# Block 1's attention maps in pairs of half-row matmuls, masks on VectorE, heads one chunk apart

## The chip, the core and the metric

The kernel runs on one core of a Trainium2 chip. The metric is the device time of one execution in microseconds. TensorE (PE, with its weight loads shown apart as PEld), VectorE (DVE), ScalarE (ACT), GpSimd (POOL) and the DMA queue of SyncE (SP) run side by side, each in its own order, and wait for each other on semaphores.

## The reference

Two transformer blocks follow each other on 256 tokens of 1024 features, all in fp32. Block 1 has two attention branches. The first is a differential attention with 4 heads: each head has two causal softmax maps over keys of 64 features, and the second is subtracted from the first, times a scalar. The second has 8 heads of 64 features; with 256 tokens in one block of 256 it is plain causal attention. Block 2 (two layers) has a retention branch with 4 heads and a stick-breaking branch with 8 heads of 128 features, and a feed-forward part.

```python
# Block 1, branch 0, for each of 4 heads and two maps m of 64 features
s = einsum('bqhmd,bkhmd->bhmqk', q, k) * scale ; s = where(key <= query, s, -inf)
a = softmax(s) ; w = a[:, :, 0] - lam * a[:, :, 1] ; o = w @ v
# Block 1, branch 1, for each of 8 heads of 64 features
s = einsum('bhqd,bhkd->bhqk', q, k) * scale ; s = where(key <= query, s, -inf) ; o = softmax(s) @ v
# Block 2, stick-breaking, for each of 8 heads and 2 layers
z = q @ k.T * scale ; causal = key < query ; lb = log_sigmoid(z) ; l1 = where(causal, lb - z, 0)
w = where(causal, exp(lb + reversed_cumsum(l1) - l1), 0) ; o = w @ v
```

## The kernel before, in words

All weights stream from HBM in 189 chunks of 128 x 2048 numbers (1 MB). fp32 numbers are split into a high and a low fp32r part (`split` for the weights: the high part on ACT, L286, the low part on DVE, L287; `hilo` for activations, L127 and L128), and a product is made of three matmuls, high by high, high by low and low by high (`mm3`, L131 to L133). A chunk of the main stream is 16 matmuls with 512 moving columns (L295) and 16 with 256 (L297), which fill one PSUM bank for each half of the chunk. The banks of the main stream are a ring of five (`acc`), those of everything else a ring of three (`aux`).

The main loop (L1007 to L1020) goes over the chunks. For chunk i it writes down the split of chunk i+2, the load of chunk i+5, then the matmuls and evacuations of chunk i, and after these one step (`next`) of every thread that was alive before chunk i. A thread is a Python generator; each `yield` puts what follows it one chunk later. This is a program order, not the order of execution: a planner with its own cost model takes, for each engine, from what is ready, and may move instructions of a later chunk ahead of those that wait. Only ScalarE's table functions (exp, sigmoid, ln) and its table loads keep the program's order among themselves, through the token in `act` (L107 to L115): when a function of the other table set comes next in program order, a table load stands before it.

`block1_branch(br)` (L546) makes q (2 chunks), k (2 chunks) and v (2 chunks) of one branch, and starts four `soft_head` threads (L462) when k is done. Each thread has two maps: in branch 0 the two maps of one head, in branch 1 two heads. The 64 features of map 0 lie on partitions 0 to 63, those of map 1 on 64 to 127. The steps of a thread:

- scores: for map 0 and then for map 1, six matmuls over 64 rows (three with 128 columns for the first 128 queries, three with 256 for the second) into a bank of `aux`, and a seventh matmul, `mask` (L458), that adds the causal mask to the two diagonal blocks by multiplying an identity with a table of 0 and -1e30. Then, for each map and each half of the queries, the maximum on DVE (L479), read from PSUM, and the exponential on ACT (L480, recorded as L114), read from PSUM. DVE makes the reciprocals and scales the result (L486, L487 in branch 0, L491 in branch 1).
- one chunk later, the turn: transposes on PE (L497) and `hilo` into the rings `ph` and `pl`.
- one chunk later, the product with v: in branch 0 nine matmuls with 128 columns (L509), then a norm of the head's output, and one chunk later a last transpose; in branch 1 six matmuls with 256 columns and six with 128 (L528, L529). The result goes to tile `A` (a1), multiplied with the gate tile `G` (g1).

Threads j = 0 and 1 take their scores two chunks behind the end of k, threads 2 and 3 three chunks behind. The program order of Block 1 is: branch 0 (chunks 0 to 5), the four gate chunks of both branches (6 to 9, `gate1`, whose sigmoids stand at chunks 7, 8 and 9), branch 1 (10 to 15), four more gate chunks (16 to 19), and at chunk 20 the first of the chunks that merge the branches (`branch1`, L611): its first half reads heads 0 to 3 of `A`, its second half heads 4 to 7. The gates wait for it in a ring of four buffers (`sig`).

In Block 2, `sb_head` (L746) uses the same `mask` helper with another table: six matmuls over 128 rows, then the mask matmul, then ACT's |z| from PSUM (L755).

Of the kernel before, what the change touches and what calls it, by code (L numbers as in the profile page):

```python
# [17 lines left out]
P = 128  # L18
# [3 lines left out]
S = 256  # L22
# [11 lines left out]
C_MQ = 704  # L34
C_MS = 832
C_TRI = 960
C_DEC = 1088
# [39 lines left out]
def tile_blocks(ctx: ExitStack, tc: tile.TileContext, a: dict, out: bass.AP):  # L77
# [66 lines left out]
    msk = tl([384], "sig", bufs=4)  # L144
# [8 lines left out]
    idr = tl([P], "idr", F32R)  # L153
    mqr = tl([P], "mqr", F32R)
    msr = tl([P], "msr", F32R)
# [7 lines left out]
    def late_consts():  # L163
        load(cst, a["tables"][:, 0:C_SB])
        load(msk, a["tables"][:, C_SB:C_DEC])
        load(lamv, a["lambdas"].rearrange("(o i e) -> o i e", o=1, e=64).to_broadcast([P, 4, 64]))

    def use_consts():
        V.tensor_mul(gfm, g_fin, g_mix[0])
        V.tensor_scalar_mul(subg, subg, 1.0 - LAM_INIT)  # L170
        V.tensor_copy(idr, ident)
        V.tensor_copy(mqr, msk[:, 0:128])
        V.tensor_copy(msr, msk[:, 128:256])
        V.tensor_copy(tri, msk[:, 256:384])
# [40 lines left out]
    def sums(sq, cols=True):  # L215
        h, l = tl([S], "ph", F32R, 4), tl([S], "pl", F32R, 4)
# [199 lines left out]
    e_slot = [scr[:, i * 768:(i + 1) * 768].rearrange("p (m q) -> p m q", m=2) for i in range(2)]  # L416
    o_slot = [scr[:, 1536 + i * 256:1536 + (i + 1) * 256].rearrange("p (h e) -> p h e", h=2) for i in range(2)]
# [37 lines left out]
    def mask(ps, m):  # L455

        o = ps.rearrange("p (b s) -> p b s", b=2)[:, :, 0:P]
        T.matmul(o, lhsT=idr, rhs=m[:, None, :].to_broadcast([P, 2, P]), start=False, stop=True, skip_group_check=True)  # L458

    BLK = ((0, 0, 0), (128, 1, 0), (256, 1, 1))  # L460

    def soft_head(idx, j, v, diff, wait):  # L462
# [3 lines left out]
        ps = [aux(), aux()]  # L466
        for m in range(2):
            r = slice(m * 64, m * 64 + 64)
            for o, q0, kn in ((0, 0, 128), (128, 128, 256)):
                q, k = slice(q0, q0 + 128), slice(0, kn)  # L470
                mm3(ps[m][:, o:o + kn], qh[r, q], ql[r, q], kh[r, k], kl[r, k], o == 0, False)
            mask(ps[m], mqr)
        e = e_slot[idx % 2]
        mx, sm = tl([4], "mx", bufs=4), tl([4], "sm", bufs=4)
        segs = ((0, 0, 128), (1, 128, 384))
        for m in range(2):
            for h, lo, hi in segs:
                i = 2 * m + h
                V.tensor_reduce(mx[:, i:i + 1], ps[m][:, lo:hi], AX.X, ALU.max, negate=True)  # L479
                act(e[:, m, lo:hi], ps[m][:, lo:hi], AF.Exp, bias=mx[:, i:i + 1], accum_out=sm[:, i:i + 1])  # L480
        rs = tl([4], "rs", bufs=4)
        V.reciprocal(rs, sm)
        if diff:
            V.tensor_scalar_mul(rs[:, 2:4], rs[:, 2:4], lam[:, 2:3])
            for h, lo, hi in segs:
                V.tensor_scalar_mul(e[:, 1, lo:hi], e[:, 1, lo:hi], rs[:, 2 + h:3 + h])  # L486
                V.scalar_tensor_tensor(e[:, 0, lo:hi], e[:, 0, lo:hi], rs[:, h:h + 1], e[:, 1, lo:hi], ALU.mult, ALU.add)  # L487
        else:
            for m in range(2):
                for h, lo, hi in segs:  # L490
                    V.tensor_scalar_mul(e[:, m, lo:hi], e[:, m, lo:hi], rs[:, 2 * m + h:2 * m + h + 1])  # L491
        yield
        wt = []
        for m in range(1 if diff else 2):
# [3 lines left out]
            h, l = tl([384], "ph", F32R, 4), tl([384], "pl", F32R, 4)  # L498
            hilo(h, l, pt[:, 0:384])
            wt.append((h, l))  # L500
# [3 lines left out]
        if diff:  # L504
            po = aux()[:, 0:S].rearrange("p (h e) -> p h e", h=2)
            h, l = wt[0]
# [16 lines left out]
        else:  # L523
            po = aux().rearrange("p (m q) -> p m q", m=2)
            for m in range(2):
                h, l = wt[m]
                vc = slice(j * P, (j + 1) * P)
                mm3(po[:, m], vh[:, 0, vc], vl[:, 0, vc], h[:, 0:256], l[:, 0:256], m == 0, False)  # L528
                mm3(po[:, m, 128:256], vh[:, 1, vc], vl[:, 1, vc], h[:, 256:384], l[:, 256:384], False, True)  # L529
# [16 lines left out]
    def block1_branch(br):  # L546
        v = Norm()
        for w_ in range(2):
            qn = []

            def qk_evac(ps, h, w_=w_, qn=qn):
# [8 lines left out]
                if w_:  # L560
                    for j in range(4):
                        threads.append(soft_head(4 * br + j, j, v, br == 0, 1 + j // 2))
# [16 lines left out]
    block1_branch(0)  # L579
    for c, b in enumerate((6, 7, 14, 15)):  # L580
        gate1(c, b)
    block1_branch(1)
# [128 lines left out]
    def ret_head(h, j, qk, v, L):  # L711
# [7 lines left out]
        dh, dl = tl([384], "ph", F32R, 4), tl([384], "pl", F32R, 4)  # L719
# [26 lines left out]
    def sb_head(h, j, qk, v, L):  # L746
# [4 lines left out]
        mm3(z[:, 256:384], kh[:, j, 128:256], kl[:, j, 128:256], qh[:, j, 128:256], ql[:, j, 128:256], False, False)  # L751
        mask(z, msr)
# [6 lines left out]
        h_, l_ = tl([384], "ph", F32R, 4), tl([384], "pl", F32R, 4)  # L759
# [7 lines left out]
        h_, l_ = tl([384], "ph", F32R, 4), tl([384], "pl", F32R, 4)  # L767
# [316 lines left out]
```

## Time and profile before

| | |
|---|---|
| time, median of 3 runs | 1178.29 us (1177.98 to 1181.79) |
| the profiled execution's own time | 1178.23 us |
| span of its trace | 1176.4 us |
| PE busy | 1161.2 us, 99% |
| DVE busy | 886.9 us, 75% |
| ACT busy | 706.7 us, 60% |
| granted TensorE clock | 0.996 of full speed |

The span reaches from the first to the last instruction of the program; 1.8 us of the profiled execution lie around it. A matmul's end in the trace is modelled and matmuls overlap, so what a matmul costs is read from the start of one to the start of the next, not from its duration.

### The profile page before, as it was taken

The numbers are of one execution on the slowest core, as the hardware profiler recorded it, in microseconds if no ns is written. First come the engines' busy times: TensorE is split into PE (matmuls) and PEld (weight loads), VectorE is DVE, ScalarE is ACT, GpSimd is POOL, SyncE is SP. The second block draws the span as 40 slices with busy tenths as digits, with TensorE's granted clock in tenths as the row PEclk, the third lists the DMA queues.
The fourth block names the chain that finished last, engine by engine and source line by source line (L and its number), as shares of the span: only waits on it lengthen the run. The fifth ranks groups of instructions, "written<-read, shape, count | busy, mean of one in ns | idle before, by whom it ended". The sixth has DMA issues, their size and how long they took to land.

```text
span 1176.4 us, 17442 instructions
## 1 busy us (share of the span) xinstructions
PE 1161.2 (99%) x6642; PEld 1011.3 (86%) x6642; DVE 886.9 (75%) x1449; ACT 706.7 (60%) x1275; POOL 230.4 (20%) x242
## 2 busy tenths in 40 slices
PE   8999999999999999999999999999999999999997
PEld 6888889997888888888888888888888888888887
DVE  6776768878989676568977777997776667867664
ACT  6657556566457776546745546556867565856452
POOL 1023104124462122202000002653112222000001
PEclk9999999999999999999999999999999999999999
DMA  8443434545335444545555555445444555555540
GB/s 309 180 143 144 146 114 160 202 180 203 144 143 179 148 163 155 190 169 185 209 191 203 180 185 217 162 161 182 159 145 157 190 191 192 184 182 199 192 179 36
DMA packets 29603, 204.47 MB, mean 174 GB/s; under 512 B 3408, under 2 KB 3664, under 8 KB 5584
## 3 DMA queue, kind: packets, MB, share of 16 engines
q1 hardware_dynamic: 29376, 203.34, 48.0%
q8 instruction: 52, 0.85, 0.3%
q14 instruction: 31, 0.25, 0.1%
q10 hardware_dynamic: 144, 0.03, 0.0%
HBM read 202.31 MB, written 1.05 MB: 173 GB/s over the span
## 4 chain that ended last, share of the span: by engine, by line
PE 93%; DVE 5%; issue 1%; ACT 0%; DMA 0%; POOL 0%; POOLq 0%; DVEq 0%; ACTq 0%
PE acc L295 41%; PE acc L297 21%; PE acc L336 19%; PE aux L131 2%; PE aux L133 2%; PE aux L132 1%; PE acc L131 1%; PE acc L132 1%; PE acc L133 1%; DVE wl L287 1%; DVE sig L801 1%; PE aux L458 1%; PE aux L764 1%; PE acc L324 1%; DMA X<-in_xt_dram 0%
## 5 line engine op out<-in xcount | busy, mean ns | idle before, releaser
L287 DVE TENSOR_TENSOR wl<-raw,wh 128x1024 fp32r<-128x1024 f32 (+1 forms) x380 | 463.2, 1253 | 154.4 <-ACT wh L286 152.2
L295 PE MATMUL acc<-X,wh 128*128 128x512 f32 x1472 | 524.7, 398 | 2.5 <-DVE vl L387 1.8
L286 ACT ACTIVATE wh<-raw 128x1024 fp32r<-128x1024 f32 (+1 forms) x380 | 380.7, 1047 | 200.2 <-PE acc L295 131.8
L297 PE MATMUL acc<-X,wl 128*128 128x256 f32 x1472 | 412.6, 281 | 0.0
L295 PEld LDWEIGHTS acc<-X,wh 128*128 128x128 f32 x1472 | 276.6, 188 | 64.5 <-DVE vl L387 2.1
L297 PEld LDWEIGHTS acc<-X,wl 128*128 128x128 f32 x1472 | 278.5, 189 | 2.3
L336 PE MATMUL acc<-wh,X 128*128 128x512 f32 x432 | 112.2, 392 | 0.0
L313 ACT ACTIVATE f<-acc 128x256 f32<-128x256 f32 x216 | 78.7, 372 | 42.2 <-PE acc L297 42.0
L314 DVE TENSOR_TENSOR f<-f,acc 128x256 f32<-128x256 f32 x216 | 86.4, 413 | 22.1 <-ACT f L313 21.3
L336 PEld LDWEIGHTS acc<-wh,X 128*128 128x128 f32 x432 | 79.7, 188 | 15.9
L295 PE MATMUL acc<-A,wh 128*128 128x512 f32 x256 | 90.2, 396 | 0.0
L295 PE MATMUL acc<-B,wh 128*128 128x512 f32 x256 | 90.1, 396 | 0.0
L207 POOL TENSOR_TENSOR sq<-sq,f 128x256 f32<-128x256 f32 x30 | 31.5, 1050 | 268.2 <-ACT f L205 267.6
L589 POOL TENSOR_TENSOR sig<-f,nr 128x256 f32<-128x256 f32 x48 | 42.5, 893 | 148.5 <-DVE f L314 148.4
L297 PE MATMUL acc<-B,wl 128*128 128x256 f32 x256 | 71.4, 279 | 0.0
L297 PE MATMUL acc<-A,wl 128*128 128x256 f32 x256 | 71.3, 279 | 0.0
L295 PE MATMUL acc<-M,wh 128*128 128x512 f32 x192 | 67.1, 397 | 0.0
L658 DVE TENSOR_TENSOR X<-X,acc 128x256 f32<-128x256 f32 x112 | 45.3, 416 | 24.8 <-PE acc L297 23.7
L336 PE MATMUL acc<-wl,X 128*128 128x512 f32 x216 | 59.5, 393 | 0.0
L295 PEld LDWEIGHTS acc<-B,wh 128*128 128x128 f32 x256 | 48.1, 188 | 11.6
L295 PEld LDWEIGHTS acc<-A,wh 128*128 128x128 f32 x256 | 48.1, 188 | 11.3
L297 PE MATMUL acc<-M,wl 128*128 128x256 f32 x192 | 52.7, 280 | 0.0
(224 smaller groups left out, 1744.6 us busy)
## 6 DMA issues: line engine op xcount, KB each, us to landing
raw<-in_wstream_dram SPq DMA_DIRECT2D x187, 1024.0 KB, 4.8
raw<-in_wstream_dram SPq DMA_DIRECT2D x4, 512.0 KB, 7.7
B<-in_tables_dram SPq DMA_DIRECT2D x2, 768.0 KB, 6.8
X<-in_xt_dram SPq DMA_DIRECT2D x2, 512.0 KB, 6.3
out_dram<-M SPq DMA_DIRECT2D x4, 256.0 KB, 2.2
M<-in_g_final_dram SPq DMA_DIRECT2D x1, 512.0 KB, 3.7
cst<-in_tables_dram SPq DMA_DIRECT2D x1, 352.0 KB, 10.0
B<-in_pt_dram SPq DMA_DIRECT2D x1, 256.0 KB, 2.7
```

What stands on the lines that cost most here:

```text
L131: T.matmul(o, lhsT=lh, rhs=rh, start=start, stop=False, skip_group_check=True)
L133: T.matmul(o, lhsT=ll, rhs=rh, start=False, stop=stop, skip_group_check=True)
L207: (V if k == KT - 1 else G).tensor_add(sq, sq, t)
L286: A.activation(ch.wh[:, k], ch.raw[:, k], AF.Copy)
L287: V.tensor_sub(ch.wl[:, k], ch.raw[:, k], f32(ch.wh[:, k]))
L295: T.matmul(ps, lhsT=ch.wh[:, k, w], rhs=x.rearrange("p c t -> p (c t)"), start=i == 0, stop=last, skip_group_check=True)
L297: T.matmul(ps[:, 0:S], lhsT=ch.wl[:, k, w], rhs=x[:, 0], start=False, stop=last, skip_group_check=True)
L313: A.activation(t, ps[:, S:2 * S], AF.Copy)
L314: V.tensor_add(t, t, ps[:, 0:S])
L336: T.matmul(p[:, 0:w], lhsT=xs[:, k, t], rhs=ws[:, i, o], start=n == 0 and k == 0, stop=n == 2 and k == KT - 1, skip_group_check=True)
L589: G.tensor_mul(store[(c, i)][0][:, k % 2], fold(ps), st.n.rb)
L658: V.tensor_add(X[:, k], X[:, k], ps[:, o:o + S])
```

## The change

- Scores: the masks' matmuls go. The twelve half-row matmuls of a thread are written as six pairs, map 0 and map 1 in turn, with the same columns, and a token keeps them in this order among themselves. Map 0 goes into an `aux` bank, map 1 into an `acc` bank.
- DVE's maximum becomes one instruction that reads the scores from PSUM and the mask from SBUF, adds them, changes the sign, writes the result to SBUF and gives the minimum of it. The exponential reads that result in SBUF, in place.
- The scaling of the exponentials goes from DVE to ACT (24 instructions; the four threads' `scalar_tensor_tensor` of branch 0 stay).
- Thread j waits 1 + j chunks, not 1 + j // 2, and there is a second `yield` between scores and turn. Four slots for the exponentials instead of two.
- Branch 1's product with v: both maps in one matmul, three with 512 and three with 256 columns.
- The rings `ph` and `pl` have two buffers of 768 instead of four of 384.
- Program order of Block 1: branch 0, two gate chunks (6, 7), branch 1 (8 to 13), two gate chunks (14, 15), and on as before.
- Block 2's stick-breaking: the mask matmul becomes an addition in PSUM on DVE; `h2`, `l2` hold both of a head's splits.

```diff
     def late_consts():
         load(cst, a["tables"][:, 0:C_SB])
-        load(msk, a["tables"][:, C_SB:C_DEC])
+        load(msk, a["tables"][:, C_SB:C_TRI])
+        load(tri_f, a["tables"][:, C_TRI:C_DEC])
...
-    def mask(ps, m):
-
-        o = ps.rearrange("p (b s) -> p b s", b=2)[:, :, 0:P]
-        T.matmul(o, lhsT=idr, rhs=m[:, None, :].to_broadcast([P, 2, P]), start=False, stop=True, skip_group_check=True)
...
         qh, ql, kh, kl = m1.h[:, j], m1.l[:, j], m1.h[:, 4 + j], m1.l[:, 4 + j]
-        ps = [aux(), aux()]
-        for m in range(2):
-            r = slice(m * 64, m * 64 + 64)
-            for o, q0, kn in ((0, 0, 128), (128, 128, 256)):
-                q, k = slice(q0, q0 + 128), slice(0, kn)
-                mm3(ps[m][:, o:o + kn], qh[r, q], ql[r, q], kh[r, k], kl[r, k], o == 0, False)
-            mask(ps[m], mqr)
-        e = e_slot[idx % 2]
+        ps = [aux(), acc()]
+        for o, q0, kn in ((0, 0, 128), (128, 128, 256)):
+            for n, (q_, k_) in enumerate(((qh, kh), (qh, kl), (ql, kh))):
+                for m in range(2):
+                    r = slice(m * 64, m * 64 + 64)
+                    mm = T.matmul(ps[m][:, o:o + kn], lhsT=q_[r, q0:q0 + 128], rhs=k_[r, 0:kn],
+                                  start=o == 0 and n == 0, stop=n == 2, skip_group_check=True)
+                    tc.stamp_issue_order_token(mm.ins, "maps")
+        e = e_slot[idx % 4]
...
-                V.tensor_reduce(mx[:, i:i + 1], ps[m][:, lo:hi], AX.X, ALU.max, negate=True)
-                act(e[:, m, lo:hi], ps[m][:, lo:hi], AF.Exp, bias=mx[:, i:i + 1], accum_out=sm[:, i:i + 1])
+                em = e[:, m, lo:hi]
+                V.tensor_tensor_reduce(em, ps[m][:, lo:hi], m_seg[h], -1.0, 3e38, ALU.add, ALU.min, mx[:, i:i + 1])
+                act(em, em, AF.Exp, scale=-1.0, bias=mx[:, i:i + 1], accum_out=sm[:, i:i + 1])
...
-                V.tensor_scalar_mul(e[:, 1, lo:hi], e[:, 1, lo:hi], rs[:, 2 + h:3 + h])
+                A.activation(e[:, 1, lo:hi], e[:, 1, lo:hi], AF.Copy, scale=rs[:, 2 + h:3 + h])
...
-                    V.tensor_scalar_mul(e[:, m, lo:hi], e[:, m, lo:hi], rs[:, 2 * m + h:2 * m + h + 1])
-        yield
-        wt = []
+                    A.activation(e[:, m, lo:hi], e[:, m, lo:hi], AF.Copy, scale=rs[:, 2 * m + h:2 * m + h + 1])
+        yield
+        yield
+        wh, wl = tl([2, 384], "ph", F32R, 2), tl([2, 384], "pl", F32R, 2)
...
-            for m in range(2):
-                h, l = wt[m]
-                vc = slice(j * P, (j + 1) * P)
-                mm3(po[:, m], vh[:, 0, vc], vl[:, 0, vc], h[:, 0:256], l[:, 0:256], m == 0, False)
-                mm3(po[:, m, 128:256], vh[:, 1, vc], vl[:, 1, vc], h[:, 256:384], l[:, 256:384], False, True)
+            vc = slice(j * P, (j + 1) * P)
+            mm3(po, vh[:, 0, vc], vl[:, 0, vc], wh[:, :, 0:256], wl[:, :, 0:256], True, False)
+            mm3(po[:, :, 128:256], vh[:, 1, vc], vl[:, 1, vc], wh[:, :, 256:384], wl[:, :, 256:384], False, True)
...
-                        threads.append(soft_head(4 * br + j, j, v, br == 0, 1 + j // 2))
+                        threads.append(soft_head(4 * br + j, j, v, br == 0, 1 + j))
...
-    block1_branch(0)
-    for c, b in enumerate((6, 7, 14, 15)):
-        gate1(c, b)
-    block1_branch(1)
+    for br, gates in ((0, (6, 7)), (1, (14, 15))):
+        block1_branch(br)
+        for c, b in enumerate(gates):
+            gate1(2 * br + c, b)
...
-        mask(z, msr)
+        zd = z.rearrange("p (b s) -> p b s", b=2)[:, :, 0:P]
+        V.tensor_add(zd, zd, m_sb)
```

## Rows read from the trace of the kernel before

**Rows 1.** The page: busy time, share of the span and instructions of each engine.

```profile
PE 1161.2 (99%) x6642; PEld 1011.3 (86%) x6642; DVE 886.9 (75%) x1449; ACT 706.7 (60%) x1275; POOL 230.4 (20%) x242
```

**Rows 2.** The page: the chain that ended last, by engine.

```profile
PE 93%; DVE 5%; issue 1%; ACT 0%; DMA 0%; POOL 0%; POOLq 0%; DVEq 0%; ACTq 0%
```

**Rows 3.** Busy time by stretch: stretch, length, PE, PEld, DVE, ACT, POOL, clock, DMA, GB/s.

```profile
44.00:125.00 81.00, 81.00 (x443) 67.72 (x443) 59.35 (x115) 53.67 (x124) 16.87 (x21) 1.00 0.42 148
125.00:180.00 55.00, 54.15 (x352) 47.38 (x351) 35.67 (x80) 30.96 (x73) 5.19 (x8) 1.00 0.32 114
260.00:360.00 100.00, 95.84 (x527) 82.21 (x525) 91.87 (x148) 58.85 (x103) 51.50 (x49) 0.98 0.43 159
360.00:440.00 80.00, 80.00 (x474) 70.74 (x472) 60.12 (x93) 59.10 (x111) 13.17 (x18) 1.00 0.45 160
```

**Rows 4.** PE in order of time, one map: start, duration, line, operation, tiles, rows*columns.

```profile
58.02 0.39 PE L295 MATMUL acc<-X,wh 128*128 128x512 f32 x1
58.34 0.32 PE L131 MATMUL aux<-M 64*128 64x128 f32 x1
58.50 0.27 PE L132 MATMUL aux<-M 64*128 64x128 f32 x1
...
59.02 0.28 PE L133 MATMUL aux<-M 64*128 64x256 f32 x1
59.22 0.38 PE L458 MATMUL aux<-mqr,idr 128*128 128x256 f32 x1
59.45 0.28 PE L297 MATMUL acc<-X,wl 128*128 128x256 f32 x1
59.56 0.40 PE L295 MATMUL acc<-X,wh 128*128 128x512 f32 x1
59.80 0.28 PE L297 MATMUL acc<-X,wl 128*128 128x256 f32 x1
```

**Rows 5.** PE in order of time where a map is broken up by the main stream.

```profile
50.54 0.32 PE L131 MATMUL aux<-M 64*128 64x128 f32 x1
50.79 0.38 PE L297 MATMUL acc<-X,wl 128*128 128x256 f32 x1
...
51.34 0.32 PE L132 MATMUL aux<-M 64*128 64x128 f32 x1
```

**Rows 6.** Block 1's mask line: count, shortest, median and longest ns, first and last start.

```profile
L458 PE MATMUL aux<-mqr,idr x16: 382/384/387, 52.1 to 156.7; 128*128 128x256 f32 x16
```

**Rows 7.** PE in order of time around a mask of Block 2.

```profile
371.28 0.27 PE L133 MATMUL aux<-M 128*128 128x128 f32 x1
371.39 0.33 PE L458 MATMUL aux<-msr,idr 128*128 128x256 f32 x1
371.56 0.28 PE L131 MATMUL aux<-M 128*128 128x256 f32 x1
```

**Rows 8.** PE in order of time, branch 1's product with v, idle time and releaser in brackets.

```profile
158.49 0.28 PE L133 MATMUL aux<-ph,vl 128*128 128x128 f32 x1
159.49 0.39 PE L131 MATMUL aux<-ph,vh 128*128 128x256 f32 x1 [0.73 <-ACT B L114]
...
160.93 0.30 PE L497 MATMUL aux<-cst,B 128*128 128x128 f32 x1
```

**Rows 9.** ACT and DVE by line and shape, 44 to 180 us: count, busy us, mean ns.

```profile
L479 DVE TENSOR_REDUCE mx<-aux 128x1 f32<-128x256 f32 x16 | 6.7, 417 | 3.5 <-ACT B L114 3.5
L112 ACT ACT_TABLE_LOAD x3 | 3.8, 1283 | 0.1
L517 ACT ACTIVATE B<-aux,ss 128x128 f32<-128x128 f32 x8 | 2.4, 387 | 1.3 <-POOL ss L515 1.3
L555 ACT ACTIVATE sig<-acc,nr 128x256 f32<-128x256 f32 x4 | 1.7, 474 | 1.3 <-PE acc L336 1.3
```

**Rows 10.** ACT in order of time around a table load.

```profile
82.63 1.28 ACT L112 ACT_TABLE_LOAD   x1
83.93 1.34 ACT L114 ACTIVATE f<-G 128x256 f32<-128x256 f32 x4
```

More of the change, by code (lines that the diff above doesn't have):

```diff
@@ L33 @@
 C_SB = 704
[L34 to L37, printed above, removed]
+C_Z = 704
+C_MQ = 832
+C_MS = 960
+C_TRI = 1088
+C_DEC = 1216
 C_ALL = C_DEC + 4 * 384
@@ L143, in tile_blocks @@
     cst = tl([C_SB], "cst")
-    msk = tl([384], "sig", bufs=4)
+    msk = tl([384], "msk")
+    tri_f = tl([P], "sig", bufs=4)
     ident = cst[:, C_ID:C_ID + P]
@@ L152, in tile_blocks @@
     V.tensor_copy(one_r, ones)
-    idr = tl([P], "idr", F32R)
-    mqr = tl([P], "mqr", F32R)
-    msr = tl([P], "msr", F32R)
+    m_seg = msk[:, P:2 * P], msk[:, 0:2 * P]
+    m_sb = msk[:, None, 2 * P:3 * P].to_broadcast([P, 2, P])
     tri = tl([P], "tri", F32R)
@@ L170, in use_consts @@
         V.tensor_scalar_mul(subg, subg, 1.0 - LAM_INIT)
[L171 to L174, printed above, removed]
+        V.tensor_copy(tri, tri_f)
         V.tensor_scalar_mul(neg1, ones, -1.0)
@@ L215, in sums @@
     def sums(sq, cols=True):
-        h, l = tl([S], "ph", F32R, 4), tl([S], "pl", F32R, 4)
+        h, l = tl([S], "ph", F32R, 2), tl([S], "pl", F32R, 2)
         hilo(h, l, sq)
@@ L415, in tile_blocks @@
     pw = scr[:, 2048:].rearrange("p (k t) -> p k t", k=KT)
-    e_slot = [scr[:, i * 768:(i + 1) * 768].rearrange("p (m q) -> p m q", m=2) for i in range(2)]
-    o_slot = [scr[:, 1536 + i * 256:1536 + (i + 1) * 256].rearrange("p (h e) -> p h e", h=2) for i in range(2)]
+    e_slot = [scr[:, i * 768:(i + 1) * 768].rearrange("p (m q) -> p m q", m=2) for i in range(4)]
+    o_slot = [scr[:, 3072 + i * 256:3072 + (i + 1) * 256].rearrange("p (h e) -> p h e", h=2) for i in range(2)]
     def start1():
@@ L497, in soft_head @@
                 T.transpose(pt[:, o:o + P], e[:, m, o:o + P], ident)
-            h, l = tl([384], "ph", F32R, 4), tl([384], "pl", F32R, 4)
-            hilo(h, l, pt[:, 0:384])
-            wt.append((h, l))
+            hilo(wh[:, m], wl[:, m], pt[:, 0:384])
         yield
@@ L505, in soft_head @@
             po = aux()[:, 0:S].rearrange("p (h e) -> p h e", h=2)
-            h, l = wt[0]
+            h, l = wh[:, 0], wl[:, 0]
             vc = slice(j * P, (j + 1) * P)
@@ L718, in ret_head @@
         V.tensor_mul(t, ps[:, 0:384], L.dec[:, 384 * h:384 * (h + 1)])
-        dh, dl = tl([384], "ph", F32R, 4), tl([384], "pl", F32R, 4)
+        dh, dl = tl([384], "ph", F32R, 2), tl([384], "pl", F32R, 2)
         hilo(dh, dl, t)
@@ L750, in sb_head @@
         mm3(z[:, 0:256], kh[:, j, 0:128], kl[:, j, 0:128], qh[:, j], ql[:, j], True, False)
-        mm3(z[:, 256:384], kh[:, j, 128:256], kl[:, j, 128:256], qh[:, j, 128:256], ql[:, j, 128:256], False, False)
-        mask(z, msr)
+        mm3(z[:, 256:384], kh[:, j, 128:256], kl[:, j, 128:256], qh[:, j, 128:256], ql[:, j, 128:256], False, True)
+        zd = z.rearrange("p (b s) -> p b s", b=2)[:, :, 0:P]
+        V.tensor_add(zd, zd, m_sb)
         zz = z[:, 0:384]
@@ L758, in sb_head @@
         V.scalar_tensor_tensor(t, zz, 0.0, t, ALU.max, ALU.add)
-        h_, l_ = tl([384], "ph", F32R, 4), tl([384], "pl", F32R, 4)
+        h2, l2 = tl([2, 384], "ph", F32R, 2), tl([2, 384], "pl", F32R, 2)
+        h_, l_ = h2[:, 0], l2[:, 0]
         hilo(h_, l_, t)
@@ L766, in sb_head @@
         act(t, zz, AF.Exp)
-        h_, l_ = tl([384], "ph", F32R, 4), tl([384], "pl", F32R, 4)
+        h_, l_ = h2[:, 1], l2[:, 1]
         hilo(h_, l_, t)
```

## The prediction

> **What bounds the kernel now.** I read the page first: PE is busy 99% of the span, DVE 75%, ACT 60% [rows 1]. Then the chain that ended last: 93% of it is PE [rows 2]. So the span is PE's work plus its few gaps, and a change is worth what it takes from PE's row of starts. Then busy time by stretch [rows 3]. Block 1's attention lies between 44 and 180 us; there PE has no idle time up to 125 us and 0.85 us of 55 after it, at full clock, while DVE is busy 95.0 of the 136 us (59.35 + 35.67) and ACT 84.6 (53.67 + 30.96). From 260 to 360 us, which the change hardly touches, DVE is busy 92 of 100 us and PE waits 4 us; from 360 to 440 us, where stick-breaking runs, PE has no idle time and DVE is busy 75%. Last I read PE in order of time, start to start, because the ends are modelled.
>
> **Maps, before.** One map's six matmuls and its mask take from 58.34 to 59.45, 1.11 us, and the way in costs 0.08 more: 58.02 to 58.34 is 0.32, while a 512-column matmul of the stream takes 0.24 (59.56 to 59.80) [rows 4]. That is 1.19 us. Block 1 has 16 such maps [rows 6]: 19.0 us. In three of them (starts near 50.5, 67.9 and 127.6) the planner put other matmuls inside; in the first, 0.80 us go from 50.54 to 51.34 [rows 5] for two stream matmuls (0.24 + 0.12) and a step of 0.16, so a break costs 0.28; three are 0.8. Sum 19.8 us.
>
> **Maps, after.** The mask, its way in (59.02 to 59.22, 0.20 for a matmul that else takes 0.12) and the second entry of each thread go. What is left are six pairs, one entry (0.08) and one exit (0.08). No pair of matmuls on different halves of the rows stands in this trace. Bounds: if the second of a pair costs nothing, a pair takes one step of 0.12 [rows 4], a thread 6 x 0.12 + 0.16 + 0.1 for the first start = 1.0 us, eight threads 8 us: 11.8 saved. If the two go one after the other at the 0.12 that half-row matmuls show, it is 12 x 0.12 + 0.16 = 1.6, eight 12.8: 7.0 saved. If each still pays what the first step shows (0.16 [rows 4]), 2.1, eight 16.6: 3.2 saved. I take the first end, 11.8: a stream matmul with 256 columns also takes 0.12 on all 128 rows (59.45 to 59.56 is 0.11), so the step is set by something other than the 128 columns of a small map, and the two halves share neither rows nor bank. It is a choice, so the second end is a rival.
>
> The Trainium skill (TensorEngine Tiling (Array Packing), Tiling Modes, Key Properties) says that tiles on different rows load weights and multiply in parallel; no run here shows it yet, and by it the saving is 11.8 us. The same section says that a change of tiling mode drains the engine; the 0.20 on the way from a map to its mask against 0.12 agrees [rows 4].
>
> **The other PE work.** Block 2's mask costs 0.17 us (371.39 to 371.56 [rows 7]); 8 heads in 2 layers make 16: 2.7 us. Branch 1's product with v takes 1.44 us in a thread (159.49 to 160.93 [rows 8]); after, three matmuls of 0.24 and three of 0.12 make 1.08: 0.36 by 4 threads, 1.4 us. PE's wait before it (158.49 to 159.49, less a matmul's 0.11 [rows 8]) ends on an exponential that still held an `aux` bank; the new maximum frees the bank on DVE, with one `aux` bank to a thread: 0.9 us goes, and nothing else is late there, as the main stream has two more chunks between k and the merge.
>
> **What is added.** All of it lies beside PE. DVE: the new maximum reads a mask too; lower bound the old 0.42 us, upper bound two passes, 0.83 [rows 9], I take 0.5; the 24 scalings that leave DVE outweigh it. Sixteen additions in PSUM of 128 x 256 at about 0.42 [rows 9] are 6.7 us over two stick-breaking stretches, in front of |z| on ACT; behind each addition stand splits and folds on DVE, and PE waits for the head only a chunk later. Cover: DVE's 25% idle [rows 3]; without it 3.3 us in each layer. ACT: 24 scalings, 12 of 0.39 and 12 of at most 0.47 [rows 9], 10.3 us. ACT's order also changes: exponentials of threads 2 and 3 of branch 0 now follow the sigmoids of chunk 7, and those of branch 1's threads 1 and 2 fall behind the sigmoids of chunks 14 and 15. Going through the program order I count seven table loads where there are three [rows 9]; four more at 1.28 are 5.1 us. ACT then has 84.6 + 10.3 + 5.1 = 100 us in a stretch of some 122: 82%. Cover is that threads turn two chunks behind their scores; the price without it is rival 3. The exponentials read SBUF instead of PSUM; I take no difference (between -0.1 and +0.1 us each, 3 us of ACT either way).
>
> The Trainium skill (ScalarE: Activation LUTs, What ACT_TABLE_LOAD costs) speaks against this order: it puts a switch at about 2.66 us with its drain. Here the load takes 1.28 and the next activation starts 0.02 us after its end [rows 10], so the row decides; by the page ACT would have 5.5 us more, and the sum would not move while the cover holds.
>
> **Nothing, with what hides it.** One load of constants more on SP's queue ahead of chunk 4's: 64 KB, at 148 GB/s [rows 3] 0.4 us, for a chunk that PE needs four chunks later. An `acc` bank goes to a map for the time to its last maximum, so the stream has four for some 3 us; the stream evacuates one bank while it fills the next. The rings `ph` and `pl` of two hold one thread in its turn and one at its product; in Block 2 a pair of heads fills both, and the next pair comes chunks later: at most one product of wait (1.4) in a few places.
>
> **The sum.** 11.8 + 2.7 + 1.4 + 0.9 = 16.8, less 0.8 for as many new breaks in maps as before: 16 us. The profiled execution took 1178.23 us, 1.8 around its span of 1176.4, and stands 0.06 from the median of 1178.29. Forecast **1162 us**, 1.4% faster.
>
> **The rivals.**
> 1. The halves of a pair don't overlap: 4.8 us of the gain is missing, 1167 us. For it: each half-row matmul here starts a step of 0.12 after the one before, whether it has 128 or 256 columns [rows 4], as if each had to wait for its weights, and two matmuls have two loads of them. Against it: those matmuls stood on the same rows.
> 2. The change doesn't do what it says: the token orders the maps among themselves, but the planner may still put stream matmuls or transposes between pairs, at 0.28 each [rows 5]. With one break after every second pair (two in a thread) 16 breaks cost 4.5 us, and pairs torn apart lose their overlap: 1167 to 1171 us.
> 3. ACT takes part of it back: in chunks 14 and 15 the two loads (2.6) and four scalings (1.7) are 4.3 us of new work on ACT in each chunk; if ACT is full there, PE stands 8.6 us: 1171 us. For it: 82% as a mean, in one queue, with the folds that free PE's banks behind the exponentials. Against it: PE had no wait in the stretch up to 125 us [rows 3].
> 4. Slower: ACT's written order starves PE. Place: chunks 7, 14 and 15, where an exponential may not pass a sigmoid of the same chunk, which waits for POOL's product, and folds wait behind both. Once PE's banks are full it stands for a chunk, 16 x (0.24 + 0.12) = 5.8 us, three times, with four loads on the path: 17.4 + 5.1 = 22.5 us, 1184.5 us. It decides from the point where the four free banks (four halves of a chunk, 11.6 us) are not evacuated in time. Against it: the planner lays ACT's other work into such gaps, and ACT is idle 18% as a mean.
>
> **How the numbers follow.** Forecast 55%, rival 1 20%, rival 2 8%, rival 3 10%, rival 4 5%, and 2% for several at once that end near no change. A measurement of this kernel can tell about 0.3%, 3.5 us, from no change. Faster by more than that (below 1174.8): 0.87; within: 0.07, half of it rival 3 when its price is half as much again; slower: 0.06. The range starts at 1157, where waits elsewhere (the 4 us from 260 to 360 [rows 3]) shrink with the new order, and goes to 1172, which takes in rivals 1 to 3 and the second end of the maps' bound; the third end (saving 3.2) gives 1170.8 and lies in it too.
>
> **What would show it.** In the profile of the changed kernel: pairs of half-row matmuls that start within some 0.05 us of each other and 0.12 from pair to pair, about 1.0 us from a thread's first to the stream's next matmul (right), or twelve even steps of 0.12 (rival 1); no L458; a PE busy time lower by 15 us or more; seven table loads up to 165 us; DVE's maximum near 0.5 us. Idle time of PE in Block 1 that ends on ACT or on a fold would show rivals 3 or 4. The prediction is wrong if pairs cost as much as two matmuls, if PE's gaps between 44 and 180 us come to over 3 us, or if the stretches around 371 and 822 us, now without gaps, get waits on the new addition.

## The result and the profile after

Kernel before and kernel after ran in turn on the same chip: 1178.55 us before (1177.98 to 1181.79), **1170.99 us after** (1169.83 to 1171.40). The ratio is 0.9927, with a 95% interval of 0.9911 to 0.9942: 7.6 us faster, where the forecast was 16. The time lies inside the range of 1157 to 1172 us that the prediction gave. The profiled execution of the kernel after took 1171.25 us, its span 1169.5.

The page of the kernel after, first the busy time, then the chain that ended last:

```profile
PE 1150.0 (98%) x6586; PEld 1001.9 (86%) x6586; DVE 879.9 (75%) x1470; ACT 719.4 (62%) x1303; POOL 228.4 (20%) x242
...
PE 90%; DVE 5%; ACT 2%; issue 1%; POOL 1%; DMA 0%; POOLq 0%; DVEq 0%; ACTq 0%
```

PE's busy time fell by 11.2 us [rows 1], but the span by only 6.9: PE's share of the chain fell from 93% to 90% [rows 2], and ACT and POOL, which had next to none, are now in it. That points at a wait of PE for work that passes through ACT and POOL. Busy time by stretch finds the place (stretch, length, PE, PEld, DVE, ACT, POOL, clock, DMA, GB/s):

```profile
44.00:125.00 81.00, 77.16 (x440) 64.43 (x440) 55.57 (x135) 58.59 (x139) 13.70 (x16) 0.96 0.39 139
125.00:172.00 47.00, 45.65 (x293) 39.97 (x292) 32.93 (x65) 38.95 (x86) 12.58 (x14) 1.00 0.35 129
```

Up to 125 us PE had no idle time and full clock [rows 3]; now it has 3.84 us idle and a mean clock of 0.96. PE's waits between 44 and 172 us, by who waits and for whom, in all, times, longest:

```profile
PE aux L516 <- ACT B L512: 3.8, 1, 3.8
PE aux L465 <- DVE ft L525: 0.8, 1, 0.8
PE aux L133 <- DVE pl L129: 0.5, 1, 0.5
```

One wait makes up three quarters. PE in order of time around it (start, duration, line, tiles, rows x columns; idle time and releaser in brackets):

```profile
102.17 0.28 PE L133 MATMUL aux<-vl,ph 128*128 128x128 f32 x1
102.29 0.27 PE L134 MATMUL aux<-vh,pl 128*128 128x128 f32 x1
106.40 0.48 PE L516 MATMUL aux<-cst,B 128*128 128x128 f32 x1 [3.84 <-ACT B L512]
```

L132 to L134 are the last head's product with v in branch 0, and L516 is the last transpose of the same head. Nothing stands between them on PE. In the kernel before, PE had the main stream there for 7.1 us, up to the first of such transposes:

```profile
101.68 0.27 PE L133 MATMUL aux<-vh,pl 128*128 128x128 f32 x1
101.79 0.91 PE L336 MATMUL acc<-wh,X 128*128 128x512 f32 x3
...
108.92 0.27 PE L521 MATMUL aux<-cst,B 128*128 128x128 f32 x1
```

By the program order the product stands behind chunk 11 and the transposes behind chunk 12. In the trace of after the stream has run ahead: the last matmul of chunk 13 starts at 101.21, ahead of the last head's product (101.45), and the first of chunk 14 at 109.13. What must happen between them is the head's norm: squares (L508) on ACT, L509 on DVE, the power (L510) on POOL, the scaling (L512) on ACT. ACT, DVE and POOL in order of time over the same stretch:

```profile
101.64 2.00 ACT L285 ACTIVATE wh<-raw 128x1024 fp32r<-128x1024 f32 x2 [1.16 <-PE acc L335]
103.56 0.26 ACT L508 ACTIVATE B<-aux 128x128 f32<-128x128 f32 x1
...
105.98 0.63 ACT L512 ACTIVATE B<-aux,ss 128x128 f32<-128x128 f32 x2 [0.66 <-POOL ss L510]
```
```profile
102.74 2.36 DVE L286 TENSOR_TENSOR wl<-raw,wh 128x1024 fp32r<-128x1024 f32 x2 [1.75 <-ACT wh L285]
105.01 0.16 DVE L509 TENSOR_SCALAR ss<-ss 128x2 f32<-128x2 f32 x1
```
```profile
105.25 0.69 POOL L510 TENSOR_TENSOR ss<-ss,mhalf 128x2 f32<-128x2 f32 x1 [10.29 <-DVE ss L509]
```

The squares queue on ACT behind a weight split until 103.56, 1.0 us after the product's end at 102.56. L509 queues on DVE behind the low part of that split until 105.01, 0.85 us after the squares' end at 104.16. The norm's own steps take the other 2.0 us, so the queues are half of the chain. From the start of PE's last matmul (102.29) to that of the transposes (106.40) it is 4.1 us. The chain was as long in the kernel before (product's end 101.95, last scaling's end 106.01), but there PE had the stream.

The stall costs more than its length. The same view by stretch, with the granted clock third from the right:

```profile
102.50:106.40 3.90, 0.06 (x1) 0.00 (x1) 3.66 (x5) 3.24 (x10) 0.69 (x1) 0.95 0.24 76
106.40:110.00 3.60, 3.60 (x15) 3.06 (x16) 2.06 (x5) 1.74 (x4) 0.00 (x0) 0.50 0.70 273
110.00:113.00 3.00, 3.00 (x11) 2.56 (x11) 0.16 (x1) 0.00 (x0) 0.00 (x0) 0.53 0.00 0
113.00:116.00 3.00, 3.00 (x24) 2.39 (x23) 1.15 (x6) 0.78 (x3) 0.73 (x1) 1.00 0.00 0
```

After 3.9 us without work PE ran at 0.50, the lower of its two levels (1.2 GHz), until about 113 us: PE is busy all the time, but a stream matmul with 512 columns and the next with 256 take 0.64 us together (110.58 to 111.22) where they take 0.35 later (113.00 to 113.35). Some 6.6 us at half speed are, by this estimate, 3.3 us lost.

The terms for the maps and for Block 2 show as the prediction meant them. A thread's maps, PE in order of time, beside [rows 4]:

```profile
53.76 0.28 PE L296 MATMUL acc<-X,wl 128*128 128x256 f32 x1
53.97 0.32 PE L465 MATMUL aux<-M 64*128 64x128 f32 x1
53.97 0.32 PE L465 MATMUL acc<-M 64*128 64x128 f32 x1
54.13 0.27 PE L465 MATMUL aux<-M 64*128 64x128 f32 x1
54.14 0.27 PE L465 MATMUL acc<-M 64*128 64x128 f32 x1
...
54.65 0.28 PE L465 MATMUL acc<-M 64*128 64x256 f32 x1
54.86 0.50 PE L294 MATMUL acc<-X,wh 128*128 128x512 f32 x1
```

The two halves of a pair start within 0.01 us of each other; from the first pair to the last it takes 0.68 us, and 0.21 to the stream's next matmul. DVE and ACT by line and shape from 44 to 172 us (count, busy us, mean ns, idle time before), beside [rows 9], and Block 2's new addition (count, shortest, median, longest ns):

```profile
L475 DVE CUSTOM_DVE_ANT_0 B<-aux,msk 128x256 f32<-128x256 f32 x8 | 3.4, 419 | 0.0
L475 DVE DVE_READ_ACCUMULATOR2_ANT mx<- 128x1 f32 x32 | 2.6, 83 | 0.0
```
```profile
L113 ACT ACT_TABLE_LOAD x7 | 9.0, 1283 | 0.1
L115 ACT ACTIVATE B<-B,mx 128x256 f32<-128x256 f32 x16 | 8.0, 498 | 0.0
```
```profile
L746 DVE TENSOR_TENSOR aux<-aux,msk x16: 422/429/433, 367.3 to 879.9; 128x256 f32<-128x256 f32 x16
```

### The profile page after: what moved, and what is told of

It is laid out like the page before. It is cut to its first block, busy times and chain, and to the rows that moved or that the text cites. A ratio compares the mean times of both kernels' runs of the same rounds, so it can differ in the third digit from the quotient of the medians.

```text
span 1169.5 us, 17360 instructions
## 1 busy us (share of the span) xinstructions
PE 1150.0 (98%) x6586; PEld 1001.9 (86%) x6586; DVE 879.9 (75%) x1470; ACT 719.4 (62%) x1303; POOL 228.4 (20%) x242
## 4 chain that ended last, share of the span: by engine, by line
PE 90%; DVE 5%; ACT 2%; issue 1%; POOL 1%; DMA 0%; POOLq 0%; DVEq 0%; ACTq 0%
PE acc L294 40%; PE acc L296 20%; PE acc L335 19%; DVE wl L286 2%; PE acc L133 1%; PE acc L134 1%; PE acc L132 1%; PE aux L134 1%; DVE sig L796 1%; PE aux L133 1%; PE aux L132 1%; PE aux L759 1%; PE acc L323 1%; ACT wh L285 1%; DVE M L129 0%
## 5 line engine op out<-in xcount | busy, mean ns | idle before, releaser
L294 PEld LDWEIGHTS acc<-A,wh 128*128 128x128 f32 x256 | 48.1, 188 | 11.2
L294 PEld LDWEIGHTS acc<-B,wh 128*128 128x128 f32 x256 | 47.8, 188 | 11.2
```

Source lines behind the costliest of these rows:

```text
L294: T.matmul(ps, lhsT=ch.wh[:, k, w], rhs=x.rearrange("p c t -> p (c t)"), start=i == 0, stop=last, skip_group_check=True)
```

## The experiments

**Theory A**: the forecast's terms hold on PE, and what is missing is this one stall with the low clock behind it. It arises because the new distances and the moved gate chunks have taken away the PE work that once lay between the last head's product and its last transposes. **Theory B**: the stall only stands for a limit elsewhere (ACT's longer queue, or pairs that give less), so removing it moves the wait to another place. **Theory C**: the new distances (1 + j, a second `yield`) are not needed, and cause the harm. All runs have a run of the kernel before beside them. "Gain in Block 1" is the time that a kernel has over the kernel before at the start of the same chunk of weights (the 38th), by the traces, each of one execution.

| run | median us | ratio, 95% interval | gain in Block 1, us |
|---|---|---|---|
| after | 1170.99 | 0.9927 (0.9911 to 0.9942) | 4.5 |
| e1_last_turn_later | 1162.65 | 0.9858 (0.9840 to 0.9876) | 12.8 |
| e10_fill_the_wait | 1168.20 | 0.9909 (0.9894 to 0.9923) | 6.7 |
| e13_no_head_norm | 1172.78 | 0.9942 (0.9918 to 0.9965) | 2.5 |
| e4_old_waits | 1172.94 | 0.9951 (0.9934 to 0.9968) | 1.2 |
| e11_later_old_waits | 1172.87 | 0.9954 (0.9935 to 0.9972) | 3.0 |
| e2_no_pairs | 1175.06 | 0.9964 (0.9951 to 0.9977) | 0.5 |
| e8_later_no_pairs | 1167.10 | 0.9901 (0.9886 to 0.9915) | 8.1 |
| e14_later_mask_on_pe | 1164.88 | 0.9879 (0.9856 to 0.9902) | 11.0 |
| e12_later_scale_dve | 1167.44 | 0.9899 (0.9883 to 0.9916) | 7.4 |
| e16_later_four_aux | 1172.92 | 0.9950 (0.9932 to 0.9968) | 12.2 |
| e3_sb_mask_only | 1175.92 | 0.9975 (0.9965 to 0.9984) | -1.2 |

**The last transposes one chunk later** (e1, below the first experiment). One line on top of the kernel after:

```diff
                 A.activation(o[:, h], po[:, h], AF.Copy, scale=ss[:, h:h + 1])
             yield
+            yield
             pt = aux()[:, 0:S]
```

> The changed kernel with one more yield in branch 0, so that the last transposes of a head's output stand two chunks behind its product with v, not one. Theory A (the missing gain is one wait: PE stands 4.0 us from 102.4 to 106.4 for the norm of the last head, then runs some 6.7 us at half clock, which costs another 3.3 us): the wait and the half clock go, PE goes on with the next gate chunk, and the time is 7.3 us lower than the changed kernel's 1171.0, about 1163.7. Rival B (PE had nothing else to run there, because v's and k's work of branch 1 was not ready, and the norm only happened to be what ended the idle time): an idle time of 3 to 4 us stays near 102 us under another name, with the half clock behind it, and the time is 1169 to 1172.

1162.65 us: 8.3 us faster than the kernel after by the medians, and 0.7 us from the forecast of 1162, which was for the kernel without this line. Busy time by stretch, then PE's waits from 44 to 172 us:

```profile
44.00:125.00 81.00, 80.98 (x484) 67.75 (x482) 59.59 (x150) 65.54 (x157) 15.24 (x18) 1.00 0.42 147
125.00:172.00 47.00, 46.44 (x308) 42.05 (x309) 36.39 (x59) 35.05 (x73) 14.63 (x13) 1.00 0.43 155
```
```profile
PE aux L465 <- DVE ft L526: 0.6, 1, 0.6
```

The stall is gone, the clock stays at 1.00, and no wait of like size takes its place: theory A, against B. The last head's product now ends earlier, with its last start at 95.59, and PE has stream matmuls from 95.71 on until the transposes at 103.28. PE's idle time in the two stretches falls from 5.2 us to 0.6. ACT is busy 100.6 of the 128 us and PE never waits for it.

**The stall filled with work** (e10). Sixteen matmuls of 512 columns, whose result nothing reads, held by a token between the last head's product and its transposes:

```diff
+            if idx == 3:
+                for _ in range(16):
+                    mm = T.matmul(pt, lhsT=one_r, rhs=one_r[:, None, :].to_broadcast([P, 4, P]), start=True, stop=True)
...
-                T.transpose(pt[:, h * P:(h + 1) * P], o[:, h], ident)
+                mm = T.transpose(pt[:, h * P:(h + 1) * P], o[:, h], ident)
...
```

> The changed kernel with 16 matmuls of 512 columns of ones put on TensorE between the product with v of branch 0's last head and the transposes of its output, into the bank that the transposes overwrite: 16 x 0.24 = 3.8 us of work that nobody needs, in the place where TensorE stood for 4.0 us. It parts the wait from the clock behind it. Theory A1 (the idle time itself costs 4.0 us and the half clock that follows costs another 3.3): the transposes start as late as before, near 106.4 us, but the clock stays full, so the time is 3.3 us lower than the changed kernel's 1171.0, about 1167.7. Rival (the fall of the clock has another cause, such as the transposes and half-row matmuls that follow): the clock falls as before and the time stays at 1171, or rises where the filler is longer than the wait.

1168.20 us: 2.8 us faster with more work. The intervals of the two ratios overlap (0.9911 to 0.9923), but every run is faster than every run of the kernel after (1167.04 to 1168.87 against 1169.83 to 1171.40), and the gain in Block 1 differs by 2.2 us. The transposes come no earlier (106.63), but PE is busy meanwhile:

```profile
102.50:106.40 3.90, 3.90 (x20) 3.18 (x19) 3.60 (x5) 3.25 (x10) 0.69 (x1) 1.00 0.27 78
106.40:110.00 3.60, 3.37 (x23) 2.81 (x22) 2.24 (x5) 1.76 (x5) 0.00 (x0) 1.00 0.67 273
```

The clock stays at 1.00, and the stretch behind has 23 matmuls instead of 15. So the 8.3 us that the one line brings are 2.2 to 2.8 of low clock and 4 of idle time; the rest, 1.5 to 2, is not told apart (the two smaller waits of the kernel after, 1.3 us together against 0.6, are part of it).

**The norm left out** (e13). The norm of branch 0's head outputs isn't computed; ACT only copies them:

```diff
-                A.activation(o[:, h], po[:, h], AF.Square, accum_out=ss[:, h:h + 1])
-            V.tensor_scalar(ss, ss, 1.0 / 128, EPS5, ALU.mult, ALU.add)
-            G.tensor_tensor(ss, ss, mhalf[:, 0:2], ALU.pow)
...
+                A.activation(o[:, h], po[:, h], AF.Copy)
```

> The changed kernel without the norm of branch 0's head outputs (no squares, no small VectorE operation, no power on GpSimd; the output is copied unscaled), so its result is not the reference's. It asks whether the length of the chain from the product with v to the last transposes makes the wait. In the changed kernel that chain ran from 102.6 to 106.4 us: on ScalarE behind a weight split until 103.6, on VectorE behind another until 105.0, then GpSimd and ScalarE until 106.4. Theory A: with the copy alone, only ScalarE's split and the copy remain, the wait is about 1.7 us instead of 4.0, and after so short a stop the clock stays full or falls for less: 1165 to 1166.5 (2.3 us of wait and up to 3.3 us of clock less, and 0.3 us of other head work). Rival (the wait is set by something else, such as a bank or the place of the step): a wait near 4 us stays at the same matmuls and the time stays at 1170 to 1171.

1172.78 us: the expectation failed. The wait of the last transposes did vanish, but the planner chose another order, with new waits at the same place and later. PE's waits, then its stretches:

```profile
PE aux L465 <- ACT M L128: 2.1, 1, 2.1
PE aux L494 <- ACT B L487: 2.1, 1, 2.1
```
```profile
106.00:108.00 2.00, 2.00 (x9) 1.72 (x10) 2.00 (x4) 0.35 (x2) 0.00 (x0) 0.68 0.22 41
108.00:110.00 2.00, 2.00 (x8) 1.71 (x8) 0.15 (x1) 0.00 (x0) 0.00 (x0) 0.50 0.88 336
```

The first one stands from 103.5 to 105.6 us: now the first maps of branch 1 wait for k's split on ACT, which a weight split holds up, again with no stream matmul between k's transposes and them, and again the clock falls. The second, of 2.1 us up to 123.06, is a turn that waits for ACT's scaling, with a clock of 0.50 from 126 to 130 us behind it. Since the order changed, this run doesn't give the norm's share of the stall; it shows that a shorter norm alone brings no time. What the stalls of both kernels share is a place where PE has several dependent steps in a row and no stream work among them; that this is their common cause is argued from the traces. Why the planner puts the steps in a row there, while weights for two chunks lie split (in the kernel after those of chunks 14 and 15 are ready at 98.96), was not shown.

**The old distances.** Theory C, on the kernel after (e4) and, second, on the first experiment (e11):

```diff
-        yield
         wh, wl = tl([2, 384], "ph", F32R, 2), tl([2, 384], "pl", F32R, 2)
...
-                        threads.append(soft_head(4 * br + j, j, v, br == 0, 1 + j))
+                        threads.append(soft_head(4 * br + j, j, v, br == 0, 1 + j // 2))
```

> The changed kernel with the old distances between steps: threads in twos (1 + j // 2) and the turn one chunk behind the scores; pairs, masks on VectorE, scaling on ScalarE and the order of the gates stay. Theory A: the last head's norm falls one to two chunks earlier, where the main stream has matmuls left to put in between, so the wait of 4.0 us and the half clock go: 1163 to 1166, if the turns find their exponentials ready. Rival C (the distances are needed, because the exponentials and their scaling on ScalarE are late for a turn one chunk behind): new idle time of PE on the turns in both branches, together as much as the 7.3 us or more, 1171 to 1176.

1172.94 us. PE's waits between 44 and 172 us:

```profile
PE aux L493 <- DVE pl L129: 4.4, 1, 4.4
PE aux L493 <- DVE B L483: 0.9, 1, 0.9
```

Two more waits, of 0.7 us each, stand on turns and maps. The wait of 3.8 us is gone, so the new distances have a part in it, and a turn (L493) waits 4.4 us in its place, again with a low clock behind it (0.56 from 120 to 130 us). Theory C falls: the old distances bring no time. The long wait isn't for an exponential: three turns run from 115.76 to 117.98, and the fourth waits for an `aux` bank until DVE has split an earlier turn's result (L129), at 121.76. Ahead of that stand 2.9 us of scalings and a 2.0 us weight split on ACT, then 2.4 us of the same split on DVE. Which of the two distances costs this, the threads' or the turn's, was not told apart.

> The kernel with the later last transposes (1162.65 us), with threads in twos (1 + j // 2) and the turn one chunk behind the scores, as in the kernel before. If the distances between steps matter for themselves (exponentials late for the turn, as in the run with the old waits alone, which stood 0.9, 0.7, 0.7 and 4.4 us on turns and maps): these waits stay and the time is 1170 to 1173. If that run's waits came only from where the last transposes stood, they go: 1163 to 1165.

In this combination the two slots for the heads' outputs are too few, so some outputs are overwritten before they are turned; the amount of work is the same. 1172.87 us, with the same 4.4 us at L493: the old distances cost this with or without the later last transposes. A kernel with the new distances and the old place of the gate chunks was not tried: in it the last head's product would fall behind the chunk that merges the branches. So the share of the moved gate chunks in the stall is not shown.

**The pairs undone.** Six matmuls of map 0, then six of map 1, into the same two banks; on the kernel after (e2) and on the first experiment (e8):

```diff
-        for o, q0, kn in ((0, 0, 128), (128, 128, 256)):
-            for n, (q_, k_) in enumerate(((qh, kh), (qh, kl), (ql, kh))):
-                for m in range(2):
-                    r = slice(m * 64, m * 64 + 64)
+        for m in range(2):
+            r = slice(m * 64, m * 64 + 64)
+            for o, q0, kn in ((0, 0, 128), (128, 128, 256)):
+                for n, (q_, k_) in enumerate(((qh, kh), (qh, kl), (ql, kh))):
```

> The changed kernel with the twelve half-row matmuls of a thread in the old order: all six of map 0, then all six of map 1; everything else stays. If the overlap of the two halves is what makes a thread's maps cheap (0.68 us from the first start to the last, 0.97 with the way in and out), twelve steps of 0.11 to 0.17 take 1.5 to 1.65 us instead of 0.97 and eight threads cost 4.2 to 5.4 us more: 1175 to 1176.5, unless the wait near 102 us shrinks by it. If the gain on the maps comes from the masks and the second way in alone, and the overlap is worth nothing, the time stays at 1171.

> The kernel with the later last transposes (1162.65 us) with the maps in the old order, six matmuls of map 0 and then six of map 1. It has no long wait near 102 us, so the price of the overlap stands alone: the maps took 7.2 us in the paired form and 10.4 in the kernel with unpaired maps (both from the first half-row start to the next full matmul), so 3.2 us, 1165.8. If unpaired maps also bring waits on banks that are held longer, 1167 or more; if the overlap gives nothing on the path, 1162.7.

1175.06 us and 1167.10 us: undoing the pairs costs 4.1 and 4.4 us. Summed over the threads, the maps (first half-row start to next full-row start) take 9.3 us in the second run against 7.2 in pairs. That is only 2 us. Another 1.8 are waits: PE's list in the second run has

```profile
PE aux L465 <- DVE ft L526: 1.6, 1, 1.6
PE aux L494 <- DVE pl L129: 0.8, 1, 0.8
```

where the paired one has 0.6 in all. And 0.9 us lie ahead of any map, in a stretch that the edit doesn't touch: the first map starts at 47.66 against 46.77, with a granted clock of 0.92 against 0.96 in the first 44 us of these two traces. Together that is the 4.7 us by which the gains in Block 1 differ, so the order itself costs 3.8. In the first run part of the loss is that the low clock behind the stall lasts longer (0.73 from 110 to 120 us, 0.86 in the kernel after). The 2 us are so few because six-and-six overlaps as well. PE in order of time in the second run, one thread:

```profile
62.01 0.55 PE L465 MATMUL aux<-M 64*128 64x128 f32 x3
62.29 0.32 PE L465 MATMUL acc<-M 64*128 64x128 f32 x1
62.39 0.33 PE L465 MATMUL aux<-M 64*128 64x256 f32 x1
62.45 0.27 PE L465 MATMUL acc<-M 64*128 64x128 f32 x1
```

The first matmul of map 1 (`acc`), the seventh in program order, starts at 62.29, ahead of the fourth of map 0 (62.39).

**Block 1's masks back on PE** (e14, on the first experiment), one matmul for each map behind the pairs (DVE still adds its mask):

```diff
...
+        for m in range(2):
+            zm = ps[m].rearrange("p (b s) -> p b s", b=2)[:, :, 0:P]
+            mm = T.matmul(zm, lhsT=idr, rhs=mqr[:, None, :].to_broadcast([P, 2, P]), start=False, stop=True, skip_group_check=True)
...
```

> The kernel with the later last transposes (1162.65 us) with Block 1's mask matmuls back behind each thread's six pairs (VectorE's addition stays, so masked places are masked twice). It gives the masks' own share of the gain on the maps. Each thread gets two full-row matmuls of 0.12 to 0.22 us, with no second way in, since they stand together behind the pairs: 0.3 to 0.45 us a thread, 2.4 to 3.6 us in all, 1165 to 1166.3. If the second way into the half-row form was the costlier part of the old masks, the lower end; if the masks lie in waits, 1162.7.

1164.88 us: sixteen mask matmuls cost 2.2 us where no step back to half rows follows them.

**Block 2's masks alone** (e3). The kernel before with this one edit:

```diff
...
-        mask(z, msr)
+        zd = z.rearrange("p (b s) -> p b s", b=2)[:, :, 0:P]
+        V.tensor_add(zd, zd, f32(msr)[:, None, :].to_broadcast([P, 2, P]))
```

> The kernel before with one part of the change: Block 2's masks are added on VectorE in PSUM; Block 1 is untouched. By the sum, 16 matmuls at 0.17 us go and nothing waits: 2.7 us less than before, 1175.8. Rival: VectorE's addition comes late behind the splits of the weights and the cumulative sums wait for it, which gives back some of it in each layer: 1177 to 1179.

1175.92 us: 2.5 us below the 1178.41 of the kernel before in the same runs (the interval, 0.16% to 0.35%, is 1.9 to 4.1 us). The traces agree: from the 38th chunk to the end this run gains 2.4 us on the kernel before, the kernel after 2.4 and the first experiment 2.5.

**The scalings back on DVE** (e12), on the first experiment, in branch 1 as in branch 0:

```diff
-                A.activation(e[:, 1, lo:hi], e[:, 1, lo:hi], AF.Copy, scale=rs[:, 2 + h:3 + h])
+                V.tensor_scalar_mul(e[:, 1, lo:hi], e[:, 1, lo:hi], rs[:, 2 + h:3 + h])
...
```

> The kernel with the later last transposes (1162.65 us), with the 24 scalings back on VectorE. Theory (the place of the scaling lies beside TensorE's work on either engine): 1162 to 1163.5. Rival (ScalarE, busy 79% between 44 and 170 us with seven table loads, costs TensorE something there): the 10 us that leave ScalarE make it 1 us or more faster, 1161.5 or less. Rival on the other side (VectorE's queue was the tighter one): slower by 1 us or more.

1167.44 us: expected level, it is 4.8 us slower (4 runs, 1164.90 to 1168.21). PE's waits:

```profile
PE aux L465 <- DVE ft L526: 2.3, 1, 2.3
PE aux L494 <- DVE pl L129: 0.8, 1, 0.8
```

Both end on DVE, where PE waits 0.6 us in all with the scalings on ACT: 2.5 us more. Behind them the clock falls to 0.50 (132 to 134 us; 0.83 over 130 to 140), which is some 1.7 us, and 1.0 us lies ahead of any map, where the edit touches nothing. DVE's mean share said that there was room; around 125 us there was none, with DVE busy 5.00 of the 5 us from 125 to 130.

**Four `aux` banks and four `acc` banks** (e16), on the first experiment (`NACC = 4` instead of 5), against its last wait:

> The kernel with the later last transposes (1162.65 us) with four aux banks and four acc banks instead of three and five. One wait is left in Block 1: the last thread's maps stand 0.7 us near 126 us for a bank that VectorE frees. If the aux ring is what is short, this wait goes and the time is 0.5 to 1 us lower, 1162; if the stream needs its fifth bank while a map holds one, new waits of the stream's first matmuls appear and the time is 1163 to 1167.

1172.92 us. Block 1 is as in the first experiment, without that wait; the loss lies in Block 2, where PE's waits from 260 to 300 us are

```profile
PE aux L132 <- ACT M L128: 3.5, 2, 1.8
PE acc L294 <- DVE vl L386: 2.5, 1, 2.5
```

These are 6.0 us, where the first experiment waits 4.8 in the same stretch, and the clock there is 0.91 against 1.00. Of the 10.3 us that the run is slower, some 3 have come by 360 us and some 4 more come between 520 and 700 us, where PE shows only 0.8 us of idle time. So the time says that the fifth `acc` bank is worth its place; by what the later part is lost is not shown.

## Why the prediction was half right

1. **Maps: right.** The rows show pairs within 0.01 us, a step of 0.11 to 0.17 from pair to pair, and with way in and out 0.97 us for a thread against 1.0. Rival 1 falls. By starts, the maps took 14.5 us before, with sixteen masks at 0.23 and sixteen ways in at 0.08 [rows 4] 19.5; after the first experiment's 7.2 and eight ways in, 7.9: 11.6 us saved, 11.8 forecast (less 0.8 for breaks). The Trainium skill (TensorEngine Tiling (Array Packing), Key Properties) says that tiles on different rows load and multiply in parallel; the rows agree, 0.01 us apart.
2. **But the pairs alone were over-credited.** The forecast's two ends, 8.0 and 12.8 us, priced the overlap of the halves at 4.8 us and took it that only pairs bring it. The halves overlap in either order, and the order by pairs is worth 2.0 us of matmul starts. Undoing the pairs costs 1.8 us more by waits behind them.
3. **Planner: right.** Other matmuls stand inside the maps at three places in the kernel after, as in the kernel before; rival 2 falls.
4. **Block 2's masks: right.** 2.7 us forecast, 2.5 measured alone. The addition takes 0.43 us, and PE stays without a gap from 356 to 436 us and from 810 to 890 (80.00 busy of 80.00 in both). Branch 1's product with v falls from 5.7 to 4.4 us by starts, 1.3 against 1.4 forecast.
5. **DVE and ACT: right in size.** Maximum 0.50 us (419 + 83 ns), seven table loads of 1.28, ACT 97.5 us in the kernel after and 100.6 in the first experiment against 100 forecast. The exponentials from SBUF take 0.03 us more than those from PSUM (498 ns against 470), inside the bound given; the scalings of 256 columns take 0.50, a little over the 0.47 given as the most. The sign that the text gave for rivals 3 and 4, idle time of PE that ends on ACT, did come, but what they say did not happen: where ACT is fullest (the first experiment) PE does not wait for it. That rival 3's 1171 us is the measured time is chance: its place was chunks 14 and 15 and its cause a full ACT; the stall is that of branch 0's last head, and ACT is idle in part of it (busy 3.24 of 3.90 us). The upper end of the range, in which the time lies, was there for rivals 1 to 3 and for maps that cost more, and none of them came: that the time is in the range is luck.
6. **The step that failed: "Nothing, with what hides it".** The prediction went through loads, banks and rings, and asked of scores and turns whether their cover of chunks held. It did not ask that of the last step of the chain: product with v, norm (ACT, DVE, POOL, ACT), last transposes. That step had kept its one chunk of distance, while the distances ahead of it had grown (the last head's product moved from chunk 8 to chunk 11 in the program order) and the gate chunks moved away. That step's chain takes 4.1 us, 1.85 of it in queues behind weight splits, and it was as long in the trace of before, where the stream covered it for 7.1 us. A term of some 4 us idle time and 2.2 to 3.3 of low clock is missing; the one-line edit that removes it gives 15.8 of the 16 us forecast (1178.41 to 1162.65 in the same runs). A smaller miss is the 0.9 us for the wait before branch 1's product, with "nothing else is late there": branch 1 of the kernel after has two waits of 0.8 and 0.5 us, and the first experiment still one of 0.6. With that term at 0.2, the terms as measured are 11.6 + 2.5 + 1.3 + 0.2 = 15.6 us, so the forecast's 16 doesn't rest on large errors that cancel.
7. **What would show it: right in the main.** The text put PE's gaps of over 3 us between 44 and 180 us as the sign of a wrong forecast; they are 5.2 us between 44 and 172. It also asked for a PE busy time lower by 15 us or more, and that came out at 11.2, with the low clock in it (15.8 in the first experiment: 1145.4 us). And the cover for the turns, two chunks of distance, is real: with one chunk, and the threads in twos, a turn waits 4.4 us (the old distances).

Not settled: why the planner leaves ready stream work behind the dependent steps at that place, what part the moved gate chunks have in it, and where the last 1.5 to 2 us of the 8.3 lie.

## What to carry to other kernels

When steps of a chain are moved later, go through the chain to its last step and write down, for each pair of dependent PE steps, which PE work lies between them and which queues the detour passes; distances counted in program order say little where a planner decides. A sum over PE's rows gives what a change can bring; here one uncovered detour decided whether it did, and its stall of some 4 us took the clock with it. If the gain is half of the sum, look for one wait before doubting the terms: here one `yield` gave the other half.

## What the runs showed of the hardware that was not expected

- Matmuls on different row halves overlap without being written in pairs: with six and six, the seventh in program order started 0.10 us ahead of the fourth (62.29 and 62.39), and a thread's twelve took 0.96 us from first to last start, against 0.68 in pairs and, as an estimate, some 1.3 for eleven even steps of 0.12.
- After 3.9 us idle the granted clock was 0.50 for some 6.6 us; after 2.1 us idle (the run without the norm) it was 0.68 and then 0.50 over the next 4 us. With PE kept busy through the wait of 3.9 us it stayed at 1.00, and 16 added matmuls made the kernel 2.8 us faster.
- Behind shorter waits the clock fell in some executions and not in others: after 0.72 us idle at 159 us it was 0.50 from 160 to 162 (Block 2's masks alone), while after 0.73 us at the same place in the kernel before, and after 1.6 us in the second run without pairs, it stayed at 1.00.
